# One product of each of seven weight pairs run first and kept in HBM, and the attention gate as a seven-product pair

## The chip, the cores and the metric

The kernel runs on one core of one Trainium2 chip. The time is device microseconds of one execution, given as the median of three; the profile is one further execution with the hardware profiler on. TensorE (PE, with its weight loads PEld), VectorE (DVE), ScalarE (ACT) and GpSimd (POOL) work side by side, SyncE (SP) issues most transfers, and each engine goes through its own instructions strictly in order.

## The reference: what is computed

Two layers act on 512 tokens of width 2048, in float32. Cut to what matters here:

```python
h = rmsnorm(x, g_pre)
z = h @ w_in                      # 2048 x 7184, split into gq gk gv gg ga aq ak av ag
log_a = log_sigmoid(ga @ w_alpha + b_alpha) / 16
o_gla = rmsnorm(gla_chunk_causal(gq, gk, gv, log_a)) * silu(gg)     # 4 heads
o_att = rmsnorm(chunk_band_attention(aq, ak, av, rel_bias)) * silu(ag)   # 8 heads
y = concatenate([o_gla, o_att]) @ w_out
x = x + rmsnorm(y, g_post)
```

`ag` is the attention gate, 1024 columns. It is needed only when a head's output is gated. All column groups but `ga` are cut into 14 blocks of 512 columns (AG0, AG1 are the attention gate), and `w_out` into four more.

## The kernel before

**Products.** Every float32 operand is split into a high part and a low rest; a product takes three matmuls (high x high, high x low, low x high). A weight *chunk* is 256 rows x 512 columns: one load of 512 KB, one cast on ScalarE for the high part (`high`, line 206), one subtraction on VectorE for the low part (`low`, line 216), then 12 matmuls of 512 columns (24 of 256 in the query/key pairs, which are computed feature-major).

**Pairs.** Blocks are taken two at a time by the Strassen-Winograd scheme: the 2048 rows are halved, the two blocks are the column halves, the 512 tokens are halved, and seven block products (P1 to P7) replace eight. Each product has four chunks (c = 0 to 3), so a pair has 28 jobs. `PROD` (line 136) is their order; "72" is product P7, chunk 2. The weight sums are made on VectorE in `high` (P5, P6 and P7, lines 200 and 202) and behind `low` of P2 (line 222); sums of the tokens are made once per layer by `token_sums`, kept in HBM (S1 to S4), and read back as `sa`. P2 multiplies the first token half's lower features (`A[1, 0, c]`) with the lower half of the first block. `fast_gemm` (line 330) runs a pair, and `finished` (line 355) combines its accumulators and passes quarters of the result to a consumer, in the order P3, P7, P2, P4.

**The gate.** The attention gate is not done as a pair. In layer two `std_gemm` runs the first token half against both blocks with all eight chunks, and then the second half: 32 jobs of 12 matmuls, each block loaded twice. The first half can begin while the last products of layer one still make the second half of the tokens. `prep_half` (line 496) normalises, turns and splits a half, chunk by chunk in the order `CO`. Gate rows go through SiLU and into HBM (`gate`, line 737), to be read by the heads.

**Order.** `stream` lists all jobs; `ahead` (line 254) keeps loads up to five jobs, casts up to four and low parts up to three jobs ahead of the running one. Weights land in rings: `raw` with five buffers, `H` with four, `wh` with four, `wl` with three, `sa` with four. Everything else (norms, attention, forget gate, GLA heads, token sums) is a list of small tasks that `pump` steps through at a rate per job; `until` pumps more when something is needed now. From this program the tile framework makes one fixed order per engine by a simulated timeline. Layer two of the `std_gemm` gate ends with `drain()`, then come the six pairs: values, two of queries and keys, GLA keys and queries, GLA values, GLA gate, and the two pairs of the output projection. Temporaries `t2` (eight buffers) are shared by nearly all tasks.

Of the kernel before, what the change touches and what calls it, by code (L numbers as in the profile page):

```python
# [33 lines left out]
def hybrid_trunk(  # L34
# [62 lines left out]
    oa_d = [{c: dram([P, 1024], f"oa{l}{c}") for c in range(4)} for l in range(L)]  # L97
    of_att = [[dram([P, 2, 512], f"fa{l}{c}") for c in range(4)] for l in range(L)]
    fac_d = [dram([P, 1024], f"fac{l}") for l in range(L)]

# [28 lines left out]
    OL = (2, 3, 0, 1, 4, 5, 6, 7)  # L129
    PAIRS = ((AV0, AV1), (QK01, QK23), (QK45, QK67), (GK, GQ), (GV0, GV1), (GG0, GG1))  # L130
    W01, W23 = (NB_IN, NB_IN + 1), (NB_IN + 2, NB_IN + 3)
# [3 lines left out]

    PROD = order("10 11 50 12 51 13 52 53 60 61 30 62 63 31 70 32 71 33 72 73 20 21 40 22 41 23 42 43")
    PROD_END = order("10 20 11 21 12 22 13 23 50 51 60 52 61 53 62 63 30 31 32 33 70 71 72 73 40 41 42 43")
    PROD_OUT = order("10 20 11 21 12 13 50 51 60 61 22 23 52 53 62 63 30 31 32 33 70 71 72 73 40 41 42 43")
    LEFT = {"P5": "S1", "P6": "S2", "P3": "S4", "P7": "S3", "P4": "A22"}
    SPARE = ("g12", "g13", "g16", "g17")  # L140
    lows, last_turn, first_high = [], [None], []
    last_cast, last_low, last_mm, last_load, last_h, last_copy = [None], [None], [None], [None], [None], [None]

    class Job:
# [14 lines left out]
        def load(self):  # L159
            k, c, p, b0, b1 = self.kind, self.c, self.pair, self.b0, self.b1  # L160
            end = b0 >= NB_IN and k != "std"
            if end:
                c = OC[c]
            top, bottom = (c + 4, c) if end else (c, c + 4)
            mid = end and b0 == W23[0] and self.l < L - 1
            if k == "std":
                self.raw = self.fetch(rtile("raw", bufs=5), b0, c)
            elif k == "P1":
                p["H", self.c] = self.fetch(rtile("H"), b0, top)
                last_h[0] = last_load[0]  # L170
            elif k == "P5":
                p["r", self.c] = self.fetch(rtile("raw", bufs=5), b1, top)
            elif k == "P6":
                p["r", self.c] = self.fetch(rtile("raw", bufs=5), b1, bottom)
            elif k == "P7":
                p["r", self.c] = p.pop(("t", self.c), None) or self.fetch(rtile("raw", bufs=5), b0, top)
            elif k == "P2" or (k == "P4" and end):
                p["r", self.c] = self.fetch(rtile("raw", bufs=5), b0, bottom)
            sums = (so_d if end else sa_d)[self.l]
            src = sums.get((LEFT.get(k), c))  # L180
            if src is not None and b0 != NB_IN and not (k == "P5" and b0 == AV0):
                until(lambda: k == "P4" or (id(sums), LEFT[k], c) in written)
                self.a = rtile("sa", (2, 512), F32R)
                with tc.issue_after(last_h[0]) if mid else nullcontext():
                    last_load[0] = nc.sync.dma_start(flat(self.a), src).ins
            if b0 == W23[0] and k == ("P6" if mid else "P5"):
                with tc.issue_after(last_h[0]):
                    p["t", self.c] = self.fetch(slot(f"a11{self.c}" if mid else SPARE[self.c], [2, 512]), b0, c + 4)

        def high(self):  # L190
            k, c, p = self.kind, self.c, self.pair
            if k == "std":
                src = self.raw
            else:
                h, r = p["H", c], p.get(("r", c))
                src = h if k in ("P1", "P5", "P6", "P4") else r
                early = k in ("P7", "P4") and self.b0 == W23[0] and self.l < L - 1
                with tc.issue_after(lows[-4 if early else -2]) if self.b0 >= NB_IN else nullcontext():
                    if k in ("P5", "P6") or (k == "P4" and self.b0 >= NB_IN):
                        nc.vector.tensor_tensor(out=h, in0=h, in1=r, op=ALU.add)  # L200
                    elif k == "P7":
                        nc.vector.tensor_tensor(out=r, in0=h, in1=r, op=ALU.subtract)  # L202
            self.src = src
            self.wh = rtile("wh", dtype=F32R)
            for z in self.parts():
                last_cast[0] = nc.scalar.copy(self.wh[:, z, :], src[:, z, :]).ins  # L206
# [121 lines left out]
    roles = ["XY", "YX"]  # L328

    def fast_gemm(l, pair, consume, rate=0.0, skip=0, feature_major=False, after=None, end=False, lag=0, ops=A):  # L330
        b0 = pair[0]
# [4 lines left out]
        if end:  # L336
            target.update(P2="Z")
        prod = (PROD_OUT if b0 == NB_IN else PROD_END) if end else PROD
        pace = Pace(rate, skip)
        keep = {}  # L340
# [14 lines left out]
        def finished(k, t):  # L355
# [6 lines left out]
            elif k == "P2":  # L362
                consume(0, 0, t, None, combine(acc[target[k]][t], keep["p1"][t], ALU.add, keep["p1"][t]))
            elif k == "P4":
                consume(0, 1, t, x_, None)

        def matmuls(job, k, c, ts):
            a = job.a
            if a is None:
                key = {"P1": (0, 0, c), "P2": (1, 0, c), "P4": (1, 1, c)}.get(k) or (LEFT[k], c)  # L370
                until(lambda: key in ops)
                a = ops[key]
            out_ps = acc[target[k]]
            fresh = k in starts and c == 0
            apart = end and (k, c) in (("P7", 3), ("P4", 0))
            for kk, some in [(kk, (t,)) for t in ts for kk in range(2)] if apart else [(kk, ts) for kk in range(2)]:
                if feature_major:
                    for ft in range(4):
                        f = slice(ft * P, (ft + 1) * P)
                        tok = slice(kk * 256, (kk + 1) * 256)  # L380
                        dst = out_ps[ft // 2][:, (ft % 2) * 256 : (ft % 2 + 1) * 256]
                        terms = ((job.wh, 0), (job.wh, 1), (job.wl, 0))
                        for m, (lhs, part) in enumerate(terms):
                            nc.tensor.matmul(  # L384
                                dst, lhs[:, kk, f], a[:, part, tok],
                                start=(fresh and kk == 0 and m == 0 and ft % 2 == 0),
                                stop=(c == 3 and kk == 1 and m == 2), skip_group_check=True,
                            )
                else:
                    for t in some:  # L390
                        tok = slice(kk * 256 + t * P, kk * 256 + (t + 1) * P)
                        terms = ((0, job.wh), (0, job.wl), (1, job.wh))
                        for m, (part, rhs) in enumerate(terms):
                            last_mm[0] = nc.tensor.matmul(  # L394
                                out_ps[t], a[:, part, tok], rhs[:, kk, :],
                                start=(fresh and kk == 0 and m == 0),
                                stop=(c == 3 and kk == 1 and m == 2), skip_group_check=True,
                            ).ins

        for k, c in prod:  # L400
# [95 lines left out]
    def prep_half(l, half, xs):  # L496
# [23 lines left out]
        base = l * 2 * KT  # L520
        for ch in CO:
            kh, c = divmod(ch, 4)
# [7 lines left out]
            half_turns.append(turn.ins)  # L530
            if kh == 0:
                while half == 0 and l and done["low"] < min(h_end + c, len(stream)):
# [202 lines left out]
    def layer(l):  # L735
# [104 lines left out]
        def raw_evac(o, ps):  # L840
            gate(0, o, ps, r0[:, o : o + 1])

        if l:
            for half in range(2):
                for q, b in enumerate((AG0, AG1)):
                    std_gemm(
                        l, b, (2 * half, 2 * half + 1), CO, operand_in, gate_evac(q), rate=1.3, lag=2 * half * q,
                    )
# [376 lines left out]
        def turn_gla(h, p):  # L1225
            ps = aux()
            for f in range(2):
                for tt in range(2):
# [3 lines left out]
                    )  # L1232
            assert p or h >= 2 or ("P2", h) in passed
            op = slot(OG[p, h], [2, 512], F32R)
# [292 lines left out]
```

## Time and profile before

| | |
|---|---|
| median of three runs | 1615.6 us (1613.22 to 1616.16) |
| profiled execution | 1613.77 us |
| its span | 1611.8 us |
| TensorE busy | 1603.2 us, 99%, 8942 matmuls |
| VectorE busy | 1272.4 us, 79% |
| ScalarE busy | 918.6 us, 57% |
| DMA, HBM read and written | 377.02 and 61.62 MB, 272 GB/s over the span |
| layer two: attention gate | 805.5 to 904.7 us |
| layer two: value pair | 904.7 to 981.2 us |
| layer two: two query/key pairs | 981.2 to 1172.1 us |
| layer two: GLA key/query, value, gate pairs | 1172.1, 1269.4, 1355.7 to 1448.4 us |
| layer two: output pairs | 1448.4, 1527.9 to the end |

The span is from the first to the last instruction; the execution's own time is a little longer. Line numbers (L394) are those of the kernel before. Names such as `wl<-raw,wh` say which tile an instruction writes and which it reads. A group's row gives its count, busy time and mean duration, and after the bar the time for which the engine stood idle just before, with what ended that. L316 are matmuls of `std_gemm`, L394 and L384 those of pairs (token-major and feature-major), L951 to L1137 those of attention and GLA.

### The profile page before, as it was taken

How to read it: one execution, taken by the hardware profiler on the slowest of the kernel's cores; microseconds unless marked ns; L12 is line 12 of the kernel's file. 1: busy time of each engine (PE TensorE's matmuls, PEld its weight loads, DVE VectorE, ACT ScalarE, POOL GpSimd, SP SyncE). 2: the span in 40 equal slices, each digit the busy share in tenths (PEclk: the TensorE clock that was granted, in tenths of full speed). 3: DMA queues.
4: the chain of work that ended last, by engine and by line, in shares of the span. 5: the costliest groups of instructions: out<-in, count | busy, mean ns of one | idle time of the engine just before them, and what ended most of it. 6: DMA issues, size and time to landing. Idle time of an engine off the chain costs nothing.

```text
span 1611.8 us, 24496 instructions
## 1 busy us (share of the span) xinstructions
PE 1603.2 (99%) x8942; PEld 1373.1 (85%) x8942; DVE 1272.4 (79%) x1647; ACT 918.6 (57%) x1509; POOL 127.4 (8%) x192
## 2 busy tenths in 40 slices
PE   9999999999999999999999999999999999999998
PEld 7888999998888777888888889999988887788886
DVE  5977777678777877998988677786786778689887
ACT  7544445657455556665796444456675555465654
POOL 0120000010000000100122000000100000101001
PEclk9999999999999999999999999999999999999999
DMA  9797686685868768689779886867858687686887
GB/s 371 257 373 264 246 305 205 226 306 171 282 214 283 265 214 319 218 307 388 268 264 365 325 292 232 303 206 243 307 206 278 224 295 250 224 301 240 331 300 207
DMA packets 133928, 438.17 MB, mean 272 GB/s; under 512 B 14404, under 2 KB 27204, under 8 KB 133776
## 3 DMA queue, kind: packets, MB, share of 16 engines
q1 hardware_dynamic: 117360, 376.78, 66.9%
q0 software_dynamic: 16160, 59.53, 10.0%
q8 instruction: 71, 1.16, 0.3%
q14 instruction: 49, 0.40, 0.1%
q10 hardware_dynamic: 288, 0.30, 0.1%
HBM read 377.02 MB, written 61.62 MB: 272 GB/s over the span
## 4 chain that ended last, share of the span: by engine, by line
PE 95%; DVE 2%; DMA 1%; ACT 1%; issue 1%; SPq 0%; POOLq 0%; ACTq 0%; DVEq 0%
PE mm L394 54%; PE mm L384 19%; PE mm L316 10%; PE ax L951 2%; PE ax L394 2%; PE ax L1137 1%; PE ax L934 1%; PE ax L758 1%; PE ax L1109 1%; PE ax L914 1%; PE ax L913 1%; PE ax L912 1%; DVE wl L216 1%; DMA bias<-in_rel_dram 0%; PE ax L976 0%
## 5 line engine op out<-in xcount | busy, mean ns | idle before, releaser
L394 PE MATMUL mm<-wh,sa 128*128 128x512 f32 x1600 | 517.3, 394 | 0.5 <-ACT wh L206 0.5
L206 ACT CAST wh<-H 128x1024 fp32r<-128x1024 f32 x256 | 268.5, 1051 | 215.9 <-PE mm L394 96.1
L216 DVE TENSOR_TENSOR wl<-H,wh 128x1024 fp32r<-128x1024 f32 x256 | 311.9, 1220 | 93.3 <-PE mm L394 35.9
L394 PEld LDWEIGHTS mm<-wh,sa 128*128 128x128 f32 x1600 | 299.5, 188 | 72.3 <-issue 8.6
L206 ACT CAST wh<-raw 128x1024 fp32r<-128x1024 f32 (+1 forms) x233 | 243.9, 1051 | 204.4 <-PE mm L394 89.3
L216 DVE TENSOR_TENSOR wl<-raw,wh 128x1024 fp32r<-128x1024 f32 (+1 forms) x233 | 282.4, 1215 | 58.6 <-PE mm L394 23.5
L394 PE MATMUL mm<-wl,sa 128*128 128x512 f32 x800 | 312.7, 391 | 0.0
L384 PE MATMUL mm<-sa,wh 128*128 128x256 f32 x1280 | 237.4, 285 | 0.0
L394 PE MATMUL mm<-wh,a 128*128 128x512 f32 x640 | 211.5, 394 | 0.0
L384 PEld LDWEIGHTS mm<-sa,wh 128*128 128x128 f32 x1280 | 200.2, 191 | 0.3
L384 PE MATMUL mm<-sa,wl 128*128 128x256 f32 x640 | 181.0, 283 | 0.0
L394 PEld LDWEIGHTS mm<-wl,sa 128*128 128x128 f32 x800 | 150.3, 188 | 30.5 <-DVE wl L216 0.7
L200 DVE TENSOR_TENSOR H<-H,raw 128x1024 f32<-128x1024 f32 x144 | 174.8, 1218 | 1.0
L394 PEld LDWEIGHTS mm<-wh,a 128*128 128x128 f32 x640 | 119.5, 188 | 24.9
L394 PE MATMUL mm<-wl,a 128*128 128x512 f32 x320 | 125.7, 393 | 0.0
L384 PEld LDWEIGHTS mm<-sa,wl 128*128 128x128 f32 x640 | 122.5, 191 | 0.0
L436 POOL TENSOR_TENSOR sm<-sm,mhalf 128x2 f32<-128x2 f32 (+2 forms) x40 | 51.3, 1283 | 762.4 <-DVE sm L961 457.3
L202 DVE TENSOR_TENSOR raw<-H,raw 128x1024 f32<-128x1024 f32 x56 | 68.5, 1223 | 49.4 <-DMA raw<-in_w_dram 49.4
L394 PE MATMUL mm<-wh,g 128*128 128x512 f32 x320 | 101.5, 391 | 0.0
L384 PE MATMUL mm<-a,wh 128*128 128x256 f32 x512 | 95.4, 285 | 0.0
L346 ACT COPY ev<-mm 128x512 f32<-128x512 f32 x104 | 60.7, 584 | 60.0 <-PE mm L394 43.3
L222 DVE TENSOR_TENSOR H<-H,raw 128x1024 f32<-128x1024 f32 x48 | 58.7, 1223 | 38.0 <-DMA raw<-in_w_dram 37.7
(257 smaller groups left out, 2324.5 us busy)
## 6 DMA issues: line engine op xcount, KB each, us to landing
raw<-in_w_dram SPq DMA_DIRECT2D x311, 512.0 KB, 5.1
sa<-S SPq DMA_DIRECT2D x184, 512.0 KB, 4.5
H<-in_w_dram SPq DMA_DIRECT2D x64, 512.0 KB, 5.2
sa<-A SPq DMA_DIRECT2D x48, 512.0 KB, 6.2
S<-g POOLq DMA_DIRECT2D x32, 512.0 KB, 9.3
sa<-oS SPq DMA_DIRECT2D x32, 512.0 KB, 5.4
oS<-g POOLq DMA_DIRECT2D x16, 512.0 KB, 4.5
oS<-sa POOLq DMA_DIRECT2D x16, 512.0 KB, 5.7
```

The source lines that it names most:

```text
L200: nc.vector.tensor_tensor(out=h, in0=h, in1=r, op=ALU.add)
L202: nc.vector.tensor_tensor(out=r, in0=h, in1=r, op=ALU.subtract)
L206: last_cast[0] = nc.scalar.copy(self.wh[:, z, :], src[:, z, :]).ins
L216: last_low[0] = nc.vector.tensor_tensor(out=self.wl[:, z, :], in0=self.src[:, z, :], in1=self.wh[:, z, :].bitcast(F32), op=ALU.subtract).ins
L222: nc.vector.tensor_tensor(out=h, in0=h, in1=self.src, op=ALU.add)
L316: nc.tensor.matmul(pss[o], a(part, kk, o) if callable(a) else a[:, part, t], rhs[:, kk, :], start=(i == 0 and kk == 0 and m == 0), stop=(i ...
L346: last_copy[0] = nc.scalar.copy(e, src[t]).ins
L384: nc.tensor.matmul(dst, lhs[:, kk, f], a[:, part, tok], start=(fresh and kk == 0 and m == 0 and ft % 2 == 0), stop=(c == 3 and kk == 1 and ...
L394: last_mm[0] = nc.tensor.matmul(out_ps[t], a[:, part, tok], rhs[:, kk, :], start=(fresh and kk == 0 and m == 0), stop=(c == 3 and kk == 1 ...
L436: nc.gpsimd.tensor_tensor(out=out_r, in0=v, in1=mhalf[:, : v.shape[-1]], op=ALU.pow)
L758: nc.tensor.matmul(ps[0:96, half * 256 : (half + 1) * 256], wga[kt // 10][:, kt % 10, :], op[:, i, (kt % 2) * 256 : (kt % 2 + 1) * 256], s ...
L951: nc.tensor.matmul(o, self.pt[i][:, j * P : (j + 1) * P], av[hd // 4, j // 2][:, j % 2, (hd % 4) * P : (hd % 4 + 1) * P], start=(j == 0), ...
```

## The change

In layer two alone, the P2 products of seven pairs (the attention gate and the six others) run first, one after another, by a new function; their accumulators are copied to SBUF and stored to HBM (`p2_d`). All of them need only the first token half's lower features, so `prep_half` makes these four chunks first. Then the attention gate runs through `fast_gemm` as a pair, and it and the six pairs run 24 jobs each, without P2 (`PROD_LATE`). P2's stored product is read back into two `t2` buffers after job "70" and combined after job "41". P4's weight sum, which stood behind P2's low part, is now made in `high` from a second load of the lower half of the first block. The rate of tasks per job is scaled by 28/24. S1 is read from SBUF by the gate pair instead of the value pair. Layer one keeps its order.

```diff
+    AG = (AG0, AG1)
+    p2_d = {pair: dram([P, 2, 512], f"p2_{pair[0]}") for pair in (AG,) + PAIRS}
...
+    PROD_LATE = [z for z in PROD if z[0] != "P2"]
+    FIRST = (AV0, AG0)
...
+            late = self.l and b0 < NB_IN
...
-            elif k == "P2" or (k == "P4" and end):
+            elif k == "P2" or (k == "P4" and (end or late)):
                 p["r", self.c] = self.fetch(rtile("raw", bufs=5), b0, bottom)
...
-            if src is not None and b0 != NB_IN and not (k == "P5" and b0 == AV0):
+            if src is not None and b0 != NB_IN and not (k == "P5" and b0 == FIRST[self.l]):
...
-                    if k in ("P5", "P6") or (k == "P4" and self.b0 >= NB_IN):
+                    if k in ("P5", "P6") or (k == "P4" and (self.b0 >= NB_IN or self.l)):
                         nc.vector.tensor_tensor(out=h, in0=h, in1=r, op=ALU.add)
...
-            stream += [Job(l, "std", c, b) for half in range(2) for b in (AG0, AG1) for c in CO]
+            stream += [Job(l, "std", 4 + c, b0) for b0, _ in (AG,) + PAIRS for c in range(4)]
...
-        for b0, b1 in PAIRS:
+        for b0, b1 in (AG,) * l + PAIRS:
             pr = {}
-            stream += [Job(l, k, c, b0, b1, pr) for k, c in PROD]
+            stream += [Job(l, k, c, b0, b1, pr) for k, c in (PROD_LATE if l else PROD)]
...
+    def early_gemm(l, pair, rate):
+        acc = [ps_mm.tile([P, W], F32, tag="mm", name=nm("mm")) for _ in range(2)]
+        pace = Pace(rate)
+        for c in range(4):
+            job = take(l, pair[0], "std", 4 + c)
+            until(lambda: (1, 0, c) in A)
+            product(job, A[1, 0, c], acc, range(2), c == 0, c == 3, pair[0] in (QK01, QK45))
+            ahead()
+            pace()
+        for t in range(2):
+            e = ev()
+            last_copy[0] = nc.scalar.copy(e, acc[t]).ins
+            nc.gpsimd.dma_start(p2_d[pair][:, t, :], e)
...
+        late = l and not end
+        prod = (PROD_OUT if b0 == NB_IN else PROD_END) if end else PROD_LATE if late else PROD
+        pace = Pace(rate * len(PROD) / len(prod), skip)
...
+                other = keep["p2"][t] if late else acc[target[k]][t]
+                consume(0, 0, t, None, combine(other, keep["p1"][t], ALU.add, keep["p1"][t]))
...
+            if late and (k, c) == ("P7", 0):
+                keep["p2"] = [t2() for _ in range(2)]
+                for t in range(2):
+                    nc.sync.dma_start(keep["p2"][t], p2_d[pair][:, t, :])
+            if late and (k, c) == ("P4", 1):
+                for t in range(2):
+                    finished("P2", t)
...
-        for ch in CO:
+        for ch in CO if half else (4, 5, 6, 7, 0, 1, 2, 3):
...
         if l:
-            for half in range(2):
-                for q, b in enumerate((AG0, AG1)):
-                    std_gemm(
-                        l, b, (2 * half, 2 * half + 1), CO, operand_in, gate_evac(q), rate=1.3, lag=2 * half * q,
-                    )
-                if half == 0:
-                    tasks.append(token_sums(l))
-                    tasks.append(forget_gate())
+            tasks.append(token_sums(l))
+            tasks.append(forget_gate())
+            for pair in (AG,) + PAIRS:
+                early_gemm(l, pair, 2.6)
+            fast_gemm(l, AG, gate_consume, rate=2.6)
```

`product` holds the matmul loops that stood inside `fast_gemm`, unchanged; `gate_consume` passes a quarter of the gate to `gate`.

More of the change, by code (lines that the diff above doesn't have):

```diff
@@ L337, in fast_gemm @@
             target.update(P2="Z")
-        prod = (PROD_OUT if b0 == NB_IN else PROD_END) if end else PROD
-        pace = Pace(rate, skip)
+        late = l and not end
+        prod = (PROD_OUT if b0 == NB_IN else PROD_END) if end else PROD_LATE if late else PROD
+        pace = Pace(rate * len(PROD) / len(prod), skip)
         keep = {}
@@ L372, in matmuls @@
                 a = ops[key]
-            out_ps = acc[target[k]]
-            fresh = k in starts and c == 0
             apart = end and (k, c) in (("P7", 3), ("P4", 0))
[L376 to L387, printed above, removed]
-                            )
[L389 to L398, printed above, removed]
+            product(job, a, acc[target[k]], ts, k in starts and c == 0, c == 3, feature_major, apart)
         for k, c in prod:
@@ L530, in prep_half @@
             half_turns.append(turn.ins)
-            if kh == 0:
+            if kh == (half == 0):
                 while half == 0 and l and done["low"] < min(h_end + c, len(stream)):
@@ L1232, in turn_gla @@
                     )
-            assert p or h >= 2 or ("P2", h) in passed
+            assert p or h >= 2 or l or ("P2", h) in passed
             op = slot(OG[p, h], [2, 512], F32R)
```

30 lines of the change are left out of this document (27 added, 3 removed).

## The prediction, made before the changed kernel was run

> **What bounds the kernel now.** I read the engine table of the page first, then the waits of TensorE from the end of layer one on, then busy time by stage of layer two.
>
> ```profile
> span 1611.8 us, 24496 instructions
> ...
> PE 1603.2 (99%) x8942; PEld 1373.1 (85%) x8942; DVE 1272.4 (79%) x1647; ACT 918.6 (57%) x1509; POOL 127.4 (8%) x192
> ```
> ```profile
> PE ax L1370 <- ACT t L1369: 1.2, 1, 1.2
> PE mm L394 <- ACT wh L206: 0.3, 1, 0.3
> PE ax L527 <- ACT g L512: 0.2, 1, 0.2
> ```
>
> The second fence is the whole list of TensorE's waits from 780 us to the end: 1.7 us in 830. So layer two is a queue of matmuls, and what counts is how many there are, as long as their operands stay ahead. Busy matmul time hides short gaps, because a matmul's end is modelled; the chain of waits tells the true pace:
>
> ```profile
> 904.68 76.53 PE mm L394 x336
> ...
> 1049.43 2.88 PE mm L384 x24
> ```
>
> 336 matmuls in a row in 76.53 us is 0.2278 us for one of 512 columns, so a chunk (12 of them) costs TensorE 2.733 us, and a pair (28 chunks) 76.5 us. A chunk of a query/key pair costs 2.88 us (24 of 256 columns). Below, columns are: stretch, its length, then busy time and (count) of PE, PEld, DVE, ACT, POOL, clock, DMA share, GB/s. The rows are the gate stage of layer two, its first pair, the fifth and the sixth pair, and the first output pair.
>
> ```profile
> 805.50:904.70 99.20, 99.05 (x484) 82.92 (x483) 80.67 (x109) 70.23 (x121) 21.71 (x40) 1.00 0.91 331
> 904.70:981.20 76.50, 76.50 (x338) 62.87 (x338) 55.54 (x50) 35.02 (x37) 0.55 (x1) 1.00 0.80 286
> ...
> 1269.40:1355.70 86.30, 86.30 (x421) 69.27 (x420) 70.73 (x88) 44.97 (x67) 5.53 (x6) 1.00 0.75 260
> 1355.70:1448.40 92.70, 92.70 (x462) 70.67 (x461) 72.98 (x97) 53.34 (x97) 8.35 (x9) 1.00 0.76 262
> 1448.40:1527.90 79.50, 79.23 (x357) 65.11 (x356) 74.28 (x87) 48.14 (x74) 7.45 (x14) 1.00 0.75 275
> ```
>
> To be seen: the granted clock is 1.00 throughout; the gate stage carries the densest traffic (331 GB/s, share 0.91); and VectorE, at 73% in the first pair, is at 93% (74.28 of 79.50) in the first output pair.
>
> **The matmuls that go.** The gate stage of layer two has 32 jobs of 12 matmuls (two token halves, two blocks, eight chunks). Afterwards it is a pair of seven products with four chunks each: 28 jobs, 4 early and 24 late. The six other pairs keep their 28 jobs; four of each only move to the front. So 4 x 12 = 48 matmuls go: 48 x 0.2278 = **10.9 us**, all on the path. Transposes, forget gate, attention and output stay as many as they were. 99.2 us of gate stage becomes 88.3 us of early products (28 jobs at 2.73 to 2.88 us beside the same 11.4 us of transposes and forget gate), and each late pair has 24 jobs, 65.6 us and its share of other work.
>
> **What the other engines get.** Prices, from the first pair's stretch:
>
> ```profile
> L216 DVE TENSOR_TENSOR wl<-raw,wh 128x1024 fp32r<-128x1024 f32 x12 | 14.6, 1220 | 3.2 <-PE mm L394 2.1 <-issue 1.1
> ...
> L206 ACT CAST wh<-raw 128x1024 fp32r<-128x1024 f32 x12 | 12.6, 1054 | 16.3 <-PE mm L394 16.2
> ...
> L200 DVE TENSOR_TENSOR H<-H,raw 128x1024 f32<-128x1024 f32 x8 | 9.8, 1220 | 0.1
> ...
> L202 DVE TENSOR_TENSOR raw<-H,raw 128x1024 f32<-128x1024 f32 x4 | 4.9, 1224 | 3.3 <-DMA raw<-in_w_dram 3.3
> L222 DVE TENSOR_TENSOR H<-H,raw 128x1024 f32<-128x1024 f32 x4 | 4.9, 1224 | 4.3 <-DMA raw<-in_w_dram 4.3
> L346 ACT COPY ev<-mm 128x512 f32<-128x512 f32 x6 | 3.5, 586 | 2.6 <-PE mm L394 2.4
> ```
>
> VectorE: the gate loses 4 low parts (-4.9 us) and gains 16 weight sums (+19.5) and 6 combinations of 128x512 (0.683 in a row further down, +4.1): +18.7 us. ScalarE: -4 casts (-4.2), +14 copies of the early products and 6 of the gate pair (20 x 0.586 = +11.7): +7.5 us. Neither lies on the path where the engine has room: in a late pair VectorE does 40 operations of 1.22 us, 48.8 us of 65.6, and the early stage has fewer low parts than the gate stage (28 against 32) and 88.3 us for about 76 us of VectorE work. The fifth pair is the densest: (70.73 - 4.9) of (86.3 - 10.9) is 87%, still under one. I cost all this at nothing; the cover is the three jobs (8.2 us) by which weights are prepared ahead.
>
> The 14 stores on the GpSimd queue are off the path (that engine is 8% busy). The 14 reloads stand on SyncE's queue ahead of weights, and each needs one of eight buffers that attention and the GLA heads use too. A load into another shared temporary, the gain row, has waited on that queue before:
>
> ```profile
> SPq L1328 <- PE ax L1229: 5.5, 1, 5.5
> ```
>
> Low end nothing; at the high end 5.5 us once in each of seven pairs, less what weights are ahead. I take nothing, since this wait appears nowhere among TensorE's.
>
> **Traffic.** Per load 0.524 MB. The gate loses 32 loads and gets 24 of weights and 16 of token sums; the first value pair loads four sums that it found in SBUF; six pairs read one quarter block twice (24): +36 loads, 18.9 MB, and 7.3 MB of early products out and back. The early stage: 99.2 us x 331 GB/s = 32.8 MB, less four loads (2.1) and the gate rows (2.1), plus 3.7: 32.3 MB in 88.3 us, 366 GB/s. What matters more is the end of each late pair: jobs 72 73 40 41 42 43 each want a weight and a token operand, 6.3 MB in 16.4 us, 384 GB/s. The kernel has run so before (same columns, ten microseconds each):
>
> ```profile
> 880.00:890.00 10.00, 10.00 (x65) 8.93 (x64) 6.76 (x9) 4.00 (x6) 2.64 (x5) 1.00 1.02 417
> 890.00:900.00 10.00, 10.00 (x51) 8.40 (x50) 4.92 (x6) 3.68 (x5) 0.57 (x1) 1.00 1.03 417
> ...
> 1510.00:1520.00 10.00, 10.00 (x45) 8.28 (x45) 10.00 (x11) 6.54 (x10) 0.00 (x0) 1.00 1.02 395
> 1520.00:1530.00 10.00, 10.00 (x46) 8.26 (x44) 5.35 (x6) 5.21 (x8) 0.00 (x0) 1.00 1.03 410
> ```
>
> 395 to 417 GB/s with 45 or 46 of the big matmuls in ten microseconds, which is the full pace. So rate is not the limit, at least not by itself. [...]
>
> **The landing of the last raw weights** is the first cost that I do count. In the first pair VectorE works in order and stands at the sum of a raw block that has not landed, with low parts queued behind it:
>
> ```profile
> 948.89 1.23 DVE L222 TENSOR_TENSOR H<-H,raw 128x1024 f32<-128x1024 f32 x1 [2.67 <-DMA raw<-in_w_dram]
> 950.03 1.22 DVE L216 TENSOR_TENSOR wl<-raw,wh 128x1024 fp32r<-128x1024 f32 x1
> ...
> 956.95 1.23 DVE L222 TENSOR_TENSOR H<-H,raw 128x1024 f32<-128x1024 f32 x1 [1.41 <-DMA raw<-in_w_dram]
> ```
> ```profile
> PEld mm L394 <- DVE wl L216: 0.6, 2, 0.4
> ```
> ```profile
> DMA to landing us min/median/max: 3.5/5.7/12.3
> ```
>
> The second fence is TensorE's weight loads waiting in that pair: the lead of the low parts is used up there, though only 0.6 us is lost. That raw block, the lower half of the first column block, is now loaded for P4, which multiplies its sum: landing, sum, cast, low in a row, where P2 multiplied the block itself and had the cast beside the sum. That is 1.05 us more (one cast), with no lead to take it. Low end: nothing, the wait falls on another chunk. High end: a cast and one more transfer in front (0.524 MB at 410 GB/s, 1.28 us) in all seven pairs, 16.3 us. I take 1.05 us in the three pairs in which no attention or GLA work slows the jobs before P7's end (gate, value, first query/key), 3.2 us; the same list of the later pairs names no low part.
>
> **The hand-over to the output projection** is the second. After the end of product P7 the last gate pair (sixth) has eight jobs left now, and four afterwards. Between P7's end and the stage's end VectorE does this beside its low parts:
>
> ```profile
> L106 DVE TENSOR_TENSOR g<-g,g 128x512 fp32r<-128x512 f32 x6 | 4.0, 687 | 2.0 <-ACT g L105 2.0
> ...
> L1201 DVE TENSOR_TENSOR g<-g,g 128x512 f32<-128x512 f32 x2 | 1.4, 683 | 0.0
> ...
> L1201 DVE TENSOR_TENSOR g<-g 128x512 f32<-128x512 f32 x2 | 1.3, 685 | 0.0
> ```
>
> These 6.7 us (turned outputs and the first sums) depend on P7 and move mostly into the first output pair, about 5 us of them; that stage has 79.5 - 74.3 = 5.2 us of VectorE idle, most of it this:
>
> ```profile
> L216 DVE TENSOR_TENSOR wl<-H,wh 128x1024 fp32r<-128x1024 f32 x16 | 19.5, 1221 | 5.0 <-ACT wh L206 4.6 <-issue 0.4
> ```
>
> Low end 0 (the idle time takes it), high end 5. I take 2.5.
>
> **Sum:** -10.9 + 3.2 + 2.5 = -5.2 us. The profiled execution took 1613.8 us (span 1611.8), so 1608.6; it is 1.8 under the median of the runs (1615.6, from 1613.2 to 1616.2), and from the median it would be 1610.4. I forecast **1609 us**.
>
> **Rivals.** (a) *The waits are hidden*: the scheduled order puts sums and low parts otherwise, and 8.2 us of preparation covers both costs. For it: 1.7 us of waiting in 830. Then -10.9, up to -9: 1603 to 1606. Chance 0.28. (b) *Nothing left*: both costs at the upper half of their bounds (8 + 4), or VectorE over its limit in the fifth pair: -10.9 + 12 = 1615, from 1612.5 to 1619. Against it: VectorE at 87% there. Chance 0.18. (c) *Slower, by the five raw buffers*: a buffer goes round in landing + sum + cast + low part, 5.7 + 1.22 + 1.05 + 1.22 = 9.2 us, and five of them feed a job every 1.84 us, under 2.73. From a landing of 10.2 us on, this loop decides. If the 384 GB/s at the end of each pair push the landing to the 12.3 us that was the longest in the first pair, the loop gives one job in 3.16 us: 0.43 us x 6 jobs x 7 pairs = 18 us, so -10.9 + 18 + 2.5 = +9.6, about 1624 us. A cap on the rate ends in the same place: at the gate stage's mean, 331 GB/s, the six jobs take 19.0 us, 2.6 more, 18 us in seven pairs. [...] Page medians of the landing speak against the loop, and the rows over 395 GB/s against the cap:
>
> ```profile
> raw<-in_w_dram SPq DMA_DIRECT2D x311, 512.0 KB, 5.1
> sa<-S SPq DMA_DIRECT2D x184, 512.0 KB, 4.5
> ```
>
> Chance 0.12, of which the cap has 0.03. (d) *It doesn't do what it says* (a stage that still runs 32 jobs, or products that the reload waits for at once): the job lists in the diff leave no room; counted in (b).
>
> **How the numbers follow.** The forecast (1606 to 1612.5) has 0.42, (a) 0.28, (b) 0.18, (c) 0.12. A change under 0.2% (3.2 us of 1615.6) can't be told from none in this kernel: faster is below 1612.4, the forecast and (a), 0.70; (b) is mostly no change, 0.18; slower over 1618.8 is (c), 0.12. The range from 1603 to 1618 leaves out (c) and the ends of (a) and (b), some 0.18.
>
> **What would show it.** The chain of the late pairs should be runs of 288 matmuls in 65.6 us, and the count of TensorE's instructions lower by 48. The landing step is right if weight loads or matmuls wait for VectorE's low part at the gate, first value and first query/key pair, 1 us each, just after P7; wrong if that list is as short as now. The hand-over is right if the first output pair has VectorE near 100% and is some 2.5 us longer than 79.5. (c) shows as a median landing of raw weights over 8 us. The forecast is wrong as a whole if the early stage, which I cost at nothing, is longer than 89 us, or if attention runs late for want of the two buffers that hold the reloaded product.

## The result, and the profile after

The changed kernel takes 1630.4 us in the median (1628.15 to 1630.66, four executions), the kernel before 1614.8 on the same chip: a ratio of 1.009, interval 1.0078 to 1.0103. It is **slower by 15.6 us**, where 5 us faster was forecast. The profiled execution is one of 1630.4 us with a span of 1628.6, so 16.8 us longer than the span before. The medians below leave out one execution, one of w2, that took 1750 us at a mean granted clock of 0.85.

The page of the changed kernel, its engine table, HBM traffic and the chain that ended last:

```profile
span 1628.6 us, 24537 instructions
...
PE 1602.7 (98%) x8894; PEld 1370.4 (84%) x8894; DVE 1289.0 (79%) x1665; ACT 923.1 (57%) x1525; POOL 135.4 (8%) x206
...
HBM read 399.57 MB, written 65.29 MB: 285 GB/s over the span
...
PE 88%; DMA 5%; DVE 4%; issue 1%; ACT 1%; SPq 0%; POOLq 0%; ACTq 0%; DVEq 0%
```

The same line of the kernel before:

```profile
PE 95%; DVE 2%; DMA 1%; ACT 1%; issue 1%; SPq 0%; POOLq 0%; ACTq 0%; DVEq 0%
```

The 48 matmuls are gone (8942 to 8894). TensorE's busy time hardly fell, though 10.9 us of work went. Some 6 us of the difference are matmuls at a granted clock of 0.50, which are busy for longer (last section); the rest can't be read from busy time, since the ends of matmuls are modelled. In the chain, transfers and VectorE had 3% before and now have 9%. That says where to look, not what is lost: y1 below has the same 5% and 4% and takes 1616.8 us.

TensorE's waits from 780 us to the end (us in total, times, longest), of which the list of before had 1.7 us:

```profile
PE mm L354 <- DMA sa<-S: 4.1, 2, 3.2
PE mm L354 <- DMA sa<-A: 3.6, 1, 3.6
PE mm L344 <- DVE ev L396: 3.2, 2, 2.8
PE mm L354 <- DVE ev L396: 3.1, 2, 2.6
...
PE mm L354 <- DVE wl L221: 1.0, 1, 1.0
```

The whole list has 18.3 us, 16.6 more than before. A few long waits make nearly all of it, not many short ones; they are for token operands (`sa`) and for VectorE's combination of a product (L396).

Busy time by stage: the early products, the gate pair, the value pair, the two query/key pairs, the three GLA pairs, the first output pair. Columns as in the prediction (clock, DMA share and GB/s last):

```profile
806.00:894.90 88.90, 88.90 (x531) 79.14 (x530) 74.42 (x104) 66.60 (x120) 23.45 (x45) 1.00 0.93 350
894.90:970.20 75.30, 69.72 (x291) 55.71 (x290) 51.13 (x47) 33.33 (x40) 4.32 (x8) 0.95 0.83 317
970.20:1035.40 65.20, 64.36 (x288) 52.62 (x287) 49.47 (x45) 28.81 (x32) 1.08 (x2) 1.00 0.93 344
1035.40:1114.10 78.70, 75.89 (x601) 74.78 (x600) 58.85 (x65) 38.45 (x53) 0.00 (x0) 0.98 0.82 294
1114.10:1208.70 94.60, 93.85 (x772) 92.71 (x771) 72.98 (x128) 56.16 (x123) 9.13 (x8) 1.00 0.77 273
1208.70:1293.30 84.60, 81.99 (x411) 68.88 (x410) 65.74 (x95) 50.06 (x93) 4.87 (x7) 1.00 0.84 293
1293.30:1381.60 88.30, 85.08 (x430) 68.52 (x429) 67.03 (x91) 47.62 (x88) 7.41 (x8) 0.98 0.77 273
1381.60:1466.10 84.50, 84.35 (x423) 63.76 (x422) 67.92 (x96) 49.16 (x96) 8.56 (x7) 1.00 0.81 282
1466.10:1544.90 78.80, 77.81 (x347) 63.84 (x346) 74.66 (x87) 48.98 (x74) 8.57 (x16) 1.00 0.81 291
```

The early stage takes 88.9 us (88.3 reckoned) at the densest traffic of all, and the first output pair 78.8 (79.5 before). The loss lies between them. Seven pairs of 24 jobs should take some 544 us: 65.6 for the gate pair, and for the six others the 543.8 us that they took before less 6 x 10.9, which is 478.4. (Four jobs of a query/key pair are 11.5 us and not 10.9, so 542.8 would be nearer.) They take 571.2. So the loss is **27 us**, against the 3.2 us that the sum allowed for there. Three stages have a clock under 1.00, which no stage had before.

Where the operands are late is read in the chain of waits at the end of the pairs. First the gate pair (start, us, what):

```profile
944.76 1.23 DVE H L205
...
946.01 0.33 SPq L160
...
946.43 12.00 DMA sa<-A
...
958.57 16.51 PE mm L354 x60
```

And the GLA value pair:

```profile
1340.61 5.25 DMA raw<-in_w_dram
...
1345.89 1.22 DVE H L205
...
1347.46 0.01 SPq L160
...
1347.57 8.10 DMA sa<-S
...
1355.80 4.57 PE mm L354 x12
```

Both show one pattern. VectorE makes the sum of a raw block (in the second pair as soon as the block lands), and only then does a buffer come free for which SyncE has been standing at the next load (L160). Behind that load, in order on the same queue, stands the token load that TensorE needs (issued at 946.43 and 1347.57), and it then takes 12 and 8 us to land; from 950 to 960 us the transport runs at 387 GB/s. TensorE is not waiting for the weight, but for the operand queued behind it.

The raw blocks are not all that holds SyncE's queue. Its longest single wait in the gate pair, 10.5 us up to 919.9, is for one of the four `sa` buffers, which TensorE has to leave first. The transport is almost idle meanwhile:

```profile
910.00:920.00 10.00, 9.50 (x42) 7.45 (x41) 7.93 (x8) 6.12 (x8) 0.00 (x0) 1.00 0.18 65
```

The kernel before has such a lull in its first pair too (138 GB/s from 915 to 925 us), and TensorE is busy throughout there. No run gave the ring `sa` more buffers, so its part in the loss is not shown.

In the first query/key pair it is VectorE that TensorE waits for:

```profile
1090.68 1.22 DVE H L205
...
1093.55 0.68 DVE ev L396
1094.24 0.60 DVE g L118
1094.84 1.13 DVE wl L221
1095.97 0.60 DVE g L109
1096.57 0.61 DVE ev L396
...
1097.27 4.61 PE mm L344 x24
```

P4 adds into the accumulators that hold P7's result, so it may not begin until L396 has read them. That combination stands behind a sum, a low part and operations of other tasks. Before, two jobs of P2 stood between P7 and P4.

Median landings of the page, over both layers (us last; before 5.1, 4.5, 5.2 and 6.2):

```profile
raw<-in_w_dram SPq DMA_DIRECT2D x323, 512.0 KB, 5.4
sa<-S SPq DMA_DIRECT2D x200, 512.0 KB, 4.5
H<-in_w_dram SPq DMA_DIRECT2D x68, 512.0 KB, 7.1
sa<-A SPq DMA_DIRECT2D x52, 512.0 KB, 8.1
```

The medians of raw blocks and of `sa<-S` hardly tell; those of `H` and `sa<-A` are up by 1.9 us each. The 12 us above is one `sa<-A` load of 52.

### The profile page after: what moved, and what is told of

It is laid out like the page before. It is cut to its first block, busy times and chain, and to the rows that moved or that the text cites. A ratio compares the mean times of both kernels' runs of the same rounds, so it can differ in the third digit from the quotient of the medians.

```text
span 1628.6 us, 24537 instructions
## 1 busy us (share of the span) xinstructions
PE 1602.7 (98%) x8894; PEld 1370.4 (84%) x8894; DVE 1289.0 (79%) x1665; ACT 923.1 (57%) x1525; POOL 135.4 (8%) x206
## 3 DMA queue, kind: packets, MB, share of 16 engines
q0 software_dynamic: 17280, 63.20, 10.5%
## 4 chain that ended last, share of the span: by engine, by line
PE 88%; DMA 5%; DVE 4%; issue 1%; ACT 1%; SPq 0%; POOLq 0%; ACTq 0%; DVEq 0%
PE mm L354 54%; PE mm L344 17%; PE mm L321 5%; DMA raw<-in_w_dram 3%; PE ax L354 2%; PE ax L980 2%; DVE wl L221 1%; PE ax L1166 1%; PE ax L1138 1%; DVE H L205 1%; PE ax L787 1%; PE ax L963 1%; DMA sa<-A 1%; PE ax L943 1%; PE ax L942 1%
## 5 line engine op out<-in xcount | busy, mean ns | idle before, releaser
L354 PE MATMUL mm<-wh,sa 128*128 128x512 f32 x1760 | 570.2, 396 | 12.3 <-DMA sa<-S 4.1
L211 ACT CAST wh<-H 128x1024 fp32r<-128x1024 f32 x272 | 284.7, 1051 | 246.1 <-PE mm L354 91.9
L221 DVE TENSOR_TENSOR wl<-H,wh 128x1024 fp32r<-128x1024 f32 x272 | 331.1, 1221 | 109.8 <-PE mm L354 41.1
L354 PEld LDWEIGHTS mm<-wh,sa 128*128 128x128 f32 x1760 | 331.3, 189 | 93.6 <-issue 17.9
L354 PE MATMUL mm<-wl,sa 128*128 128x512 f32 x880 | 346.0, 393 | 1.0 <-DVE wl L221 1.0
L211 ACT CAST wh<-raw 128x1024 fp32r<-128x1024 f32 (+1 forms) x213 | 223.9, 1054 | 165.4 <-PE mm L354 73.4
L221 DVE TENSOR_TENSOR wl<-raw,wh 128x1024 fp32r<-128x1024 f32 (+1 forms) x213 | 258.2, 1216 | 54.6 <-PE mm L354 29.5
L354 PE MATMUL mm<-wh,a 128*128 128x512 f32 x704 | 230.1, 393 | 0.0
L205 DVE TENSOR_TENSOR H<-H,raw 128x1024 f32<-128x1024 f32 x180 | 218.7, 1219 | 12.5 <-DMA raw<-in_w_dram 11.4
L354 PEld LDWEIGHTS mm<-wl,sa 128*128 128x128 f32 x880 | 166.2, 189 | 34.9 <-DVE wl L221 2.1
L344 PEld LDWEIGHTS mm<-a,wh 128*128 128x128 f32 x512 | 79.8, 191 | 1.2 <-ACT wh L211 0.8
## 6 DMA issues: line engine op xcount, KB each, us to landing
S<-g POOLq DMA_DIRECT2D x32, 512.0 KB, 10.5
```

The source lines that it names most:

```text
L221: last_low[0] = nc.vector.tensor_tensor(out=self.wl[:, z, :], in0=self.src[:, z, :], in1=self.wh[:, z, :].bitcast(F32), op=ALU.subtract).ins
L344: nc.tensor.matmul(dst, lhs[:, kk, f], a[:, part, tok], start=(fresh and kk == 0 and m == 0 and ft % 2 == 0), stop=(final and kk == 1 and ...
L354: last_mm[0] = nc.tensor.matmul(out_ps[t], a[:, part, tok], rhs[:, kk, :], start=(fresh and kk == 0 and m == 0), stop=(final and kk == 1 a ...
```

## The experiments

Sixteen kernels, by question. The kernel before had medians of 1614.4 to 1614.9 us beside them. "Excess" below is the length of the seven late pairs over 543.8 us, in the profile of that kernel. The kernels x2, x3, y4 and w3 compute other numbers than they should and serve to price a part; they, x4 and z4 have a single execution, and the executions of one kernel lie up to 7 us apart (y1).

### Which operand of P4 costs

P4 has two loads per job, a second raw block and a token operand. One run takes the token loads away (the operands stay in SBUF, in four buffers that are free after the early products), one the second weight load, one both.

```diff
# x1: A22 loaded once, then kept
-            if src is not None and b0 != NB_IN and not (k == "P5" and b0 == FIRST[self.l]):
+            if src is not None and b0 != NB_IN and not (k == "P5" and b0 == FIRST[self.l]) and not (k == "P4" and late):
...
+            drain()
+            for c in range(4):
+                A[1, 1, c] = slot(f"a12{c}", [2, 512], F32R)
+                nc.sync.dma_start(flat(A[1, 1, c]), sa_d[l]["A22", c])
# x2: no second load, the sum is H + H
-            elif k == "P2" or (k == "P4" and (end or late)):
+            elif k == "P2" or (k == "P4" and end):
...
+                if k == "P4" and self.l and self.b0 < NB_IN:
+                    r = h
```

> After the early products, P4's four token operands are loaded once into the four buffers that P2's operands have left, and P4 of all seven pairs reads them there: 24 fewer token loads in layer two, and no token load in the last four jobs of a pair. Theory (transport): at a pair's end two loads per job and the next pair's weights fill the transport, P4's token operand lands 8 to 14 us after its issue, and TensorE waits for it; with these loads gone the 28 us by which the seven pairs are longer than their matmuls fall to under 8, so 1605 to 1611 us. Rival (reload: the buffers and the queue places that the stored product takes): still within 4 us of 1630. Rival (sum: the second block must be summed before its cast, as predicted): within 6 us of 1630.

> P4's weight sum is made, but from data at hand (H + H), and the second load of the block is left out, so P4 multiplies other numbers than it should: 28 fewer weight loads in layer two, the same work on VectorE. Theory (transport): 1603 to 1611 us, as above, since the token operands no longer share the last jobs with weights. Rival (sum): within 6 us of 1630, since the chain sum, cast, low part stays. Rival (reload): within 4 us of 1630.

> x1_resident and x2_sum_no_load together: P4 takes its token operands from SBUF and makes its sum without a second load (H + H in its place, so other numbers): 52 loads fewer than the changed kernel. If the 13 us that x2 still lost against a full matmul pace are late operands, about 1604 to 1608, which is what the matmul count alone gives (1614.8 - 10.9 = 1604). If they are the denser VectorE, ScalarE and GLA work beside 24 jobs, 1613 to 1617, as x2.

Measured: x1 1633.0 us (ratio 1.0117, 1.0098 to 1.0137), no gain. x2 1616.8, one execution, 13.6 us under the changed kernel. w3 1610.8, one execution, 6.0 under x2. So the second weight load is worth half of the loss, and the token loads cost only once it is away. (x1 and w3 also finish all waiting tasks before the gate pair, with `drain()`; the early stage of w3 is 88.8 us, so that costs nothing there.) With the token loads gone alone, the waits moved on. In x1 TensorE waits thus:

```profile
PE mm L354 <- DMA sa<-S: 4.2, 4, 2.8
PE mm L344 <- DVE ev L396: 3.1, 2, 2.7
PE mm L354 <- DVE wl L221: 3.0, 4, 1.1
PE mm L354 <- DVE ev L396: 2.5, 2, 1.6
```

The excess is 27.4 us in the changed kernel, 12.1 in x2 and 6.9 in w3. w3 is still 6.9 us above 1603.9, which is the kernel before less 10.9. Its list of TensorE's waits has 7.4 us, 5.7 more than before, the longest 1.7 us for `sa<-S`; which order or buffer is behind them isn't settled.

### Is it the reload, or the order of the loads

```diff
# x3: the stored product is not read back
-                other = keep["p2"][t] if late else acc[target[k]][t]
+                other = keep["p1"][t] if late else acc[target[k]][t]
# x4: the next pair's P1 and P5 loads stand behind this pair's last token load
+                with tc.issue_after(last_token[0]) if self.l and last_token[0] is not None else nullcontext():
                     p["H", self.c] = self.fetch(rtile("H"), b0, top)
```

> The early products are computed and stored, but not read back; the copy of P1 is added to itself in their place, so one quarter of each block is other numbers. 14 fewer loads of 256 KB and two temporaries free. Theory (transport): 3.7 MB less of 99 MB in the late pairs, so 2 to 5 us less than 1630. Rival (reload): 1605 to 1612 us.

> The same transfers; only the first weights of the next pair (P1 and P5) are put behind the last token load of P4 on SyncE's queue. If the number of bytes is what counts (transport), the wait moves to the next pair's first jobs and the time stays within 6 us of 1630. Rival (order: weights not yet needed go ahead of tokens that are): 1608 to 1618 us.

Measured, one execution each: x3 1630.1, x4 1628.2. The reload costs nothing in the end, although it is in the chain of the changed kernel at the end of one GLA pair (a load of 7.59 us there). In x3 the wait at that place, 2.6 us, is gone, but waits for `sa<-A` come to 7.2 us over the other pairs, against 3.6. The order between two pairs is worth some 2 us, no more than executions of one kernel differ by.

### Is it P4's wait for the accumulators

y1 puts P4 directly behind P7 in the kernel before; y2 gives P4 fresh accumulators in the changed kernel (for 14 more copies on ScalarE and 14 more combinations on VectorE); y3 and y4 are y2 with x1 and with x2.

```diff
# y1, on the kernel before
-    PROD = order("... 72 73 20 21 40 22 41 23 42 43")
+    PROD = order("... 72 20 73 40 21 22 41 23 42 43")
# y2
+        if late:
+            target.update(P4="Y")
+            starts.append("P4")
...
+                consume(0, 1, t, None, combine(y_, keep["x"][t], ALU.add, keep["x"][t]))
```

> The kernel before, with one job of each pair moved: in the order of all twelve pairs P4's first chunk follows P7's last one at once (72 20 73 40 21 22 instead of 72 73 20 21 40 22). Same matmuls, transfers and sums. Theory (accumulator): P4 adds into the accumulators that VectorE must read for P7's result first, and the two jobs of P2 between them were the cover; without them each pair waits 0.6 to 2.9 us as in the changed kernel: 1622 to 1640 us. Rival (transport alone): within 4 us of 1615.

> The changed kernel, with P4 in the second pair of accumulators (free since P2 left) and started fresh: ScalarE copies P7's sum out, VectorE adds it to P4 at the end. 14 more copies of 0.58 us on ScalarE, 14 more combinations of 0.68 us on VectorE, no wait of P4 for VectorE. Theory (accumulator): the 7.6 us of waits named after VectorE's combination and the 1.7 us of half clock behind one of them go: 1618 to 1624 us. Rival (transport alone): the wait goes over to the next operand that is late, 1627 to 1632 us.

> Both: P4 fresh in the second accumulators, and its four token operands resident in SBUF for all seven pairs. Theory (accumulator and transport, two causes one behind the other, so that taking away one alone shows little): 1611 to 1619 us. If the accumulator is the only one: as y2. If transport is the only one: as x1, 1630 to 1633 us.

> P4 fresh in the second accumulators, and its weight sum from data at hand without the second load (other numbers than it should have). Theory (two causes): 4 to 8 us under the 1616.8 of the kernel with the load left out alone, so 1608 to 1613 us. Transport alone: 1615 to 1618 us.

Measured: y1 1616.8 (ratio 1.0014, 1.0005 to 1.0024, ten executions), some 2 us in twelve pairs. y2 1631.6 (1.0106, 1.0091 to 1.0121), y3 1628.9 (1.0089, 1.0072 to 1.0105), y4 1616.2, one execution, as x2. The accumulator wait is real where it stands in the chain, and removing it gains nothing: in y2 the list names no L396 any more, and other operands are late. y2 is not a clean removal, since it adds work on ScalarE and VectorE, and its longest wait, 4.5 us, is for a cast that stood behind both (a combination, then two operations of ScalarE). With y1, where the order alone costs 2 us, this theory fell as the main cause. TensorE's longest waits in y2:

```profile
PE mm L354 <- ACT wh L211: 5.0, 2, 4.5
PE mm L354 <- DMA sa<-A: 4.3, 2, 3.6
```

### Is it the ring of five raw buffers

z1 leaves all bytes in place and gives P4's second load four buffers of its own. z2 is z1 with y2. w2 is z1 with that load issued at the P3 jobs, which load no weight; w4 is w2 without the factor 28/24 on the rate of other tasks.

```diff
# z1
+            elif k == "P4" and late:
+                p["r", self.c] = self.fetch(slot(f"a12{self.c}", [2, 512]), b0, bottom)
# w2: the same load, at P3
+            if k == "P3" and late:
+                p["b", self.c] = self.fetch(slot(f"a12{self.c}", [2, 512]), b0, bottom)
# w4, with w2
-        pace = Pace(rate * len(PROD) / len(prod), skip)
+        pace = Pace(rate, skip)
```

> The changed kernel, with P4's second weight load landing in the four buffers that P2's token operands have left, instead of in the ring of five raw buffers. Same transfers, same sums, no byte less. Theory (ring): the ring of five raw buffers, which must now go round 16 times in 24 jobs instead of 28 and waits for VectorE each time, is what the second loads cost; with 12 rounds per pair the time comes near that of the kernel without these loads, 1612 to 1620 us. Rival (bytes): the transport itself is what the second loads fill, so 1626 to 1633 us.

> The same, and P4 fresh in the second accumulators. Theory (ring, and the accumulator behind it): 1608 to 1616 us, some 4 us under the kernel with own buffers alone. If own buffers change nothing: 1626 to 1633 us here too.

> z1_own_buffers (P4's second load in four buffers of its own), with that load issued at the P3 jobs, which load no weight otherwise, instead of at the P4 jobs; same bytes in each pair. If the crowding of two loads in each of the jobs 72 73 40 41 42 43 is what z1 still pays, the time falls below z1's 1622.8 to about 1612 to 1617 (the 6 us of the gate pair and 3 of the second query/key pair go). If bytes of the pair as a whole or the denser work beside it is the rest, it stays at 1620 to 1624.

> w2_own_at_P3 with the rate of other tasks per job as it was with 28 jobs (not times 28/24), so that attention and GLA work is spread over more jobs and ends later. If denser work beside the late pairs is a cost of its own (GV and GG lost 7 us in x2 and z1), 3 to 7 us below w2. If not, w2's time, or more, when the last heads then come late for the output pairs.

Measured: z1 1622.8 (ratio 1.0051, 1.0036 to 1.0066), 7.6 us under the changed kernel, about half of what leaving the loads out gives. z2 1629.3 (1.009, 1.0073 to 1.0107): fresh accumulators cost 6.5 us here, probably by the work that they add on VectorE and ScalarE. w2 1625.5, three executions (1.007, 1.005 to 1.009): moving the load away from the last jobs doesn't help (in its profile the GLA value pair ran at a clock of 0.96, where z1 has 1.00). But it moved the crowd rather than thinned it: with the load at P3, all twelve jobs from 60 to 73 have two loads each, 384 GB/s again. So w2 leaves open whether crowding is the other half. w4 1623.9 (1.0055, 1.004 to 1.007), 1.6 us under w2.

TensorE's waits in z1:

```profile
PE mm L356 <- DMA sa<-S: 3.6, 3, 2.3
PE mm L356 <- DVE wl L223: 1.9, 3, 0.7
PE mm L346 <- DMA sa<-S: 1.3, 1, 1.3
PE mm L356 <- DMA sa<-A: 1.3, 2, 0.9
```

No wait is over 2.3 us any more, the accumulator's are down to 0.2 (a row further down), and the excess is 17.2 us, not 27.4. So the ring is a cause. It probably made VectorE late too: in the changed kernel VectorE stands 11.4 us (895 to 1470 us) at P5, P6 and P4 sums of blocks that have not landed, with the combination queued behind, and z1's list has no such wait. It is not a cost by itself, since the kernel before stands 20.7 us at the sums behind P2 and loses nothing.

### Does the second load cost by itself

w1 puts this one part into the kernel before: same 28 jobs, same gate stage.

```diff
-            elif k == "P2" or (k == "P4" and end):
+            elif k == "P2" or (k == "P4" and (end or self.l)):
...
-                    if k in ("P5", "P6") or (k == "P4" and self.b0 >= NB_IN):
+                    if k in ("P5", "P6") or (k == "P4" and (self.b0 >= NB_IN or self.l)):
```

> The kernel before with one part of the change alone: in the six pairs of layer two, P4's weight sum is made in `high` from a second load of the block that P2 has just multiplied (24 more loads of 512 KB), while the 28 jobs, their order and the gate stay. If second loads cost by themselves (x2_sum_no_load and z1_own_buffers put them at 14 us over seven pairs, 2 us each), about +12 us: 1627. If they cost only where 24 jobs carry what 28 carried, because P4 then lies directly behind P7 and the ring of five has no jobs without a new sum in it, 1615 to 1618, as the kernel before.

Measured: 1615.6 us, ratio 1.0 (0.9991 to 1.0009, ten executions). **The second load costs nothing where a pair has 28 jobs.** The value pair and the first GLA pair of w1:

```profile
905.00:981.20 76.20, 76.20 (x338) 63.03 (x337) 55.67 (x51) 35.00 (x37) 0.54 (x1) 1.00 0.83 312
...
1173.40:1270.80 97.40, 97.40 (x498) 82.23 (x498) 71.20 (x104) 59.64 (x113) 4.66 (x6) 1.00 0.74 267
```

Same lengths as before (76.5 and 97.3), with 312 GB/s where there were 286. So it is the taking away of P2's jobs from the pair that makes it dear. Nor is it the demand on the ring of raw buffers alone: w1 asks one raw block per job for ten jobs running, the changed kernel for six. From the job lists: after "71 33" w1 asks 16 loads in 10 jobs (P2 needs no token load), 307 GB/s at 2.733 us a job; the changed kernel 12 loads in 6 jobs, 384 GB/s. Which property of the missing jobs matters most, their time or their single load, was not tried apart.

### Fewer early products

z3 runs five pairs with early products and leaves GLA values and gate at 28 jobs; z4 adds y2.

```diff
+    EARLY = (AG,) + PAIRS[:4]
```

> The changed kernel with five early products instead of seven: the last two pairs (GLA values and GLA gate) keep all 28 jobs as before, with no stored product and no second load. Early stage 20 jobs. Theory (each late pair costs by itself): the excess of those two pairs and of the stage behind them goes, 8 to 10 us, so 1620 to 1624 us. Rival (the cost is in the start of the gate pair and in the density of the early pairs alone): 1628 us or more, also if 20 early jobs do not cover the second half of the tokens.

> The same with P4 fresh in the second accumulators in the five late pairs: 0 to 8 us under the kernel with five early products. Theory (accumulator counts once the raw ring has room): no difference here, since the ring is as full as before in the five late pairs.

Measured: z3 1634.4 (ratio 1.0124, 1.0109 to 1.014), z4 1631.7, one execution. Worse, and at another place: from about the end of the 20 early jobs, 873 us, to 900 us TensorE stands still for 6.6 us in z3 and 6.1 us in z4, at the start of the gate pair, where the changed kernel stands for 0.5 in its first 27 us. In z3 the longest of these waits, 4.6 us, is for the cast of a block `H` that took 11.2 us to land; ahead of it in the chain stand the store of a token sum and the splitting of tokens. So 20 jobs are probably too short a cover for the second half of the tokens and the token sums.

Of the changed kernels that do the whole computation z1 is the best, and none beats the kernel before.

## Why the prediction was wrong

- **The matmuls that go: right.** 48 fewer, early stage 88.9 us (88.3; 89.1 by the prediction's own prices, since eight of its jobs are query/key jobs at 2.88), value pair 65.2 (65.6). The 10.9 us were gained, and lost again.
- **What the other engines get: right in size.** VectorE rose by 16.6 us (18.7 reckoned), ScalarE by 4.5 (7.5). That it lies off the path holds for its sum and not for its order: L396 and the sums stand in the chain at the ends of pairs.
- **The reload at nothing: right** (x3).
- **Traffic: bytes right, conclusion wrong.** 438.6 MB became 464.9, the 26.2 MB reckoned. From four rows at 395 to 417 GB/s with TensorE at full pace I took it that rate isn't the limit. Those rows show that transfers can run so, not that an operand issued late in such traffic lands in time: the loads in the chains took 8.1 and 12.0 us. The early stage at 350 GB/s lost nothing: TensorE was busy for all of its 88.9 us.
- **The landing of the last raw weights: the step that failed.** I priced it as one cast late in three pairs, 3.2 us, with 16.3 in all seven as the high end. The late pairs lost 27 us. The place was right (just after P7), the mechanism wrong: the mark that I gave for it, waits for low parts at the gate, first value and first query/key pair, is missing, and the one of 1.0 us in the list stands in the first output pair. In the chains the raw block's wait holds a buffer of the ring, the ring holds SyncE, SyncE holds the token load, and VectorE holds the combination that P4 waits for. Of the 27 us, the list of waits shows 16.6 and the lower clock some 6.2 (last section), for which the sum had no term. x2 ties about 14 to the second load, z1 about half of that to the ring, and w3 another 6 to the token loads, which the prediction costed at nothing with the traffic. w1 shows that the term should have been built on the load in a pair of 24 jobs, not on the load.
- **The hand-over, 2.5 us: wrong.** The first output pair has VectorE at 95% (74.66 of 78.80) and is no longer than before.
- **Rival (c)** named the five raw buffers and 1624 us, and got 0.12. Its place and half of its mechanism hold. Its form doesn't: it is not every job that slows, and its mark, a median landing over 8 us, isn't there (5.4 on the page). I used medians against it, and what was late in the chains were single long landings. The cap in it, at 331 GB/s, is not borne out: the windows around the falls of the clock in the last section ran at 408 to 417 GB/s.

Settled: that second loads cost where a pair has 24 jobs, and that half of this is the ring, by x2, z1 and w1. Still open: the other half (transport, or the order on the queue), the ring of token buffers, the 6.9 us that w3 keeps, and why single remedies other than z1 gain nothing, beyond that the next operand is as late.

## What to carry to other kernels

Jobs that need few operands can be what lets the queues catch up. Here the same second loads cost nothing beside P2's jobs and about 14 us without them, though every average left room. Before such a move, count the loads of the densest run of jobs and follow one buffer of the ring and what stands behind it in order on the issuing queue, with the longest landing of the trace and not the median. When several operands are late by about the same time, taking one of them away can show nothing (x1, x3): give the whole group room, or test the part alone in the kernel before.

## What the hardware showed that was not expected

After three of its waits TensorE is granted half the clock (0.50). Windows of the changed kernel around two of these waits, and in the last two rows around one after which the clock stayed (clock third from last):

```profile
957.40:960.80 3.40, 2.23 (x5) 1.82 (x6) 0.00 (x0) 0.22 (x1) 0.00 (x0) 0.50 1.02 417
960.80:964.20 3.40, 3.40 (x9) 2.64 (x8) 0.51 (x1) 0.82 (x1) 0.00 (x0) 0.50 1.03 416
1094.00:1097.30 3.30, 0.53 (x6) 0.35 (x4) 3.30 (x6) 1.77 (x4) 0.00 (x0) 1.00 1.03 408
1097.40:1100.80 3.40, 3.40 (x17) 3.40 (x18) 2.80 (x4) 1.05 (x2) 0.00 (x0) 0.50 1.04 414
...
1274.00:1277.00 3.00, 2.79 (x16) 2.16 (x14) 0.39 (x2) 1.22 (x2) 0.00 (x0) 1.00 1.07 384
1277.00:1280.00 3.00, 0.60 (x3) 0.52 (x4) 3.00 (x6) 1.22 (x4) 0.00 (x0) 1.00 1.04 397
```

The second row has 9 matmuls of 512 columns in 3.4 us, where the full pace gives 15. The half clock lasts 6.8 us after the longest wait (3.6 us), 3.4 us after the second, and comes a third time at 1356.8 us, for 3.4 us again: 13.6 us in all. TensorE was busy for 12.4 of them, so about 6.2 us are lost beside the waits themselves. A wait of 3 us that ends so costs nearly 5.

The length of the wait doesn't decide it: after 2.6 us (last two rows) the clock stayed at 1.00, and so it did after 2.3 us in the profile of z1, where every late pair runs at 1.00, but in x2 it fell after 2.1 us (mean 0.83 from 1340 to 1350 us). The falls of the changed kernel, at 957.43, 1097.37 and 1356.79 us, are 139.95 and 259.41 us apart, 41 and 76 times 3.413 us, which is also how long the half clock lasted after 1097.37 and after 1356.79. With 805 to 1545 us of this profile cut into steps of that length, one of which ends at each fall, TensorE stood for 2.47, 2.77 and 2.42 us in the three steps that end at a fall, and for 1.49 us at most in any other. The 2.6 us that did nothing lay across two steps, 1.49 us in one and 1.12 in the next. That is one profile; whether the same steps hold in those of the other kernels is not shown.
